# The last 256 gate and up columns of each feed-forward layer by seven products, and the decay columns in one tile

## The chip, the cores and the metric

The kernel runs on one core of a Trainium2 chip. The metric is the device time of one execution in microseconds (us): 586.07 us as the median of 3 runs (585.33 to 586.32). A profile of one execution stands beside it; its rows are those quoted below. The engines are PE (TensorE, matrix products), PEld (its weight loads), DVE (VectorE), ACT (ScalarE), POOL (GpSimd) and SP (SyncE, which here only starts transfers).

## The reference: what is computed

Two layers on 256 tokens of width 1024 in float32. Layer 0 mixes tokens by gated linear attention: one product with `w_in` gives queries, keys, values, a gate and 16 low-rank columns `gk_low`; `log_sigmoid(gk_low @ w_gk + b_gk) / 16` is the decay. Layer 1 mixes by softmax attention. Both end alike:

```python
def swiglu_ffn(x, w_gu, w_down):
    gate, up = jnp.split(x @ w_gu, 2, axis=-1)
    return (jax.nn.silu(gate) * up) @ w_down

x = layer_norm(DEEPNORM_ALPHA * x + y, ln_g[i, 0], ln_b[i, 0])
x = layer_norm(DEEPNORM_ALPHA * x + swiglu_ffn(x, ffn_w_gu[i], ffn_w_down[i]), ln_g[i, 1], ln_b[i, 1])
```

The hidden width is 2816, so `w_gu` has 2816 gate and 2816 up columns and `w_down` has 2816 rows (22 blocks of 128, called d0 to d21).

## The kernel before

**Split numbers.** A float32 matrix is held as a rounded high part (name ending in `h`, a CAST of ACT) and a low part (ending in `l`, a TENSOR_TENSOR subtraction of DVE). A product takes three matmuls: high by high, low by high, high by low (`mm3`, L301 to L303). So each 512 KB weight tile costs one pass of ACT and one of DVE over 128x1024 beside its matmuls.

**Who sets the order.** Every operation is handed to a small planner (`Plan`, L64). It has a cost for each operation, gives each weight tile one of 41 slots and each product one of 8 PSUM banks, plays the engines forward, and writes the program in the order that comes out. On the chip each engine then follows its own list in that order and waits on semaphores. A load on SP's queue waits until the last reader of its slot is done.

**A feed-forward layer** (`ffn`, L468) goes through the hidden columns in six blocks, `"PSSSSH"`. `P` (`plain`) and `S` (`seven`) take 512 gate and 512 up columns. `seven` sees the 256 tokens and the 1024 inputs as 2x2 halves and forms the products in Strassen's manner: seven half products instead of eight, named A to G after their weight tiles, 12 matmuls of 512 columns for each of a tile's two units. Its price is on DVE: three sums of weights (`add_to`, L571), and one sum that a transfer from POOL's queue makes while it lands (`add_dma`, L577). The tokens come out as rows, so a result is transposed on PE (L316) before the down product. `H` (`half`, L620) takes the last 256 gate and up columns: four weight tiles g50, g51, u50, u51, 96 matmuls of 256 columns that give the result already transposed, no sums.

**The down product** adds each of d0 to d21 onto four banks: `fy00`, `fy01` (tokens 0 to 127, the two halves of the output) and `fy10`, `fy11` (tokens 128 to 255). Rows of a block are added while the next block runs (`down_now`). Those of the last `S` block (d16 to d19) wait with those of `H` (d20, d21) for the end: all six for the first tokens, the layer norm of these on DVE, all six for the others, the second layer norm.

**The decay columns** (L728 to L740): the 16 columns of `gk_low` lie in two tiles, high and low, padded with zeros to 128 columns per input block, and take 24 matmuls of 256 columns. The sum is copied to `gkT`, to which row 16 (ones, for the bias) belongs.

**The start of layer 0**, after the decay: keys and queries (`gk0`, `gk1`, `gq`), then `qd` = queries times decay (L793, DVE), scores `sc` (L832, PE), a POOL copy of `qd` into `kx` (L815), and the cross scores `scx` (L842, PE), which wait for that copy.

Of the kernel before, what the change touches and what calls it, by code (L numbers as in the profile page):

```python
# [16 lines left out]
P = 128  # L17
# [174 lines left out]
def kernel(ctx, tc, x, positions, gla_w_in, gla_w_gk, gla_b_gk, gla_norm_g, gla_w_out,  # L192
# [31 lines left out]
    wgk = fixed("wgk", (GLA_RANK + 1, 512))  # L224
    gkT = fixed("gkT", (GLA_RANK + 1, S))
# [84 lines left out]
    def transpose_split(src, dst, t, half, skey=None, dstf=None, dkey=None, n=4, keep=None):  # L310
# [13 lines left out]
        def hi():  # L324
            nc.scalar.copy(view(0), ps.f.rearrange("p (k c) -> p k c", k=4))  # L325

        def lo():
            h, l = view(0), view(1)
            nc.vector.tensor_tensor(out=l, in0=ps.f.rearrange("p (k c) -> p k c", k=4), in1=h.bitcast(F32),  # L329
                                    op=ALU.subtract)  # L330
        kh = dkey if dkey is not None else (t, half)
        if dstf is None:
            act(512, hi, [ps], [(dst, ("h",) + kh)], urgent=True)
            dve(512, lo, [ps, (dst, ("h",) + kh)], [(dst, ("l",) + kh)], urgent=True)
# [133 lines left out]
    def ffn(i, xs, T, gb, dstT, last, x32):  # L468
# [6 lines left out]
        def down(k, t, bufs, f, ws, hfs=(0, 1)):  # L475
# [6 lines left out]
            pe(3 * 512 * len(hfs), g, list(bufs) + list(ws), [y[t][hf] for hf in hfs])  # L482
# [30 lines left out]
        def down_now(items):  # L513
            for k, bufs, f in items:
                ws = w_row(f"d{k}", wd, k)
                for t in range(2):
                    down(k, t, bufs, f, ws)

        def plain(b, c0, pend):
# [16 lines left out]
            return [(c0 // P + k, (h, l), lambda j=k: (hv(h)[:, j, :], hv(l)[:, j, :])) for k in range(4)]  # L536

        def seven(b, c0, pend):
# [3 lines left out]
            e1, e2 = S_("e1"), S_("e2")  # L542

            def product(ps, left, ws, first, last_):
                st, rd = lhs(left)
                for q, (wh, wl) in enumerate(ws):
                    def f(q=q, wh=wh, wl=wl):
                        for j in range(2):
                            sh, sl_ = st(2 * q + j)
                            cs = slice(512 * j, 512 * j + 512)  # L550
                            nc.tensor.matmul(ps.f, sh, wh.r[:, cs], start=first and q == 0 and j == 0, stop=False,  # L551
# [569 lines left out]
```

## Time and profile before

| | |
|---|---|
| median of 3 runs | 586.07 us |
| the profiled execution | 585.35 us, span 583.6 us |
| PE busy | 572.5 us (98% of the span), 3004 matmuls |
| DVE busy | 504.6 us (86%) |
| ACT busy | 345.7 us (59%) |
| POOL busy | 42.7 us |
| granted TensorE clock | 0.997 |

The span runs from the first to the last instruction; the time of the execution has 1.75 us more around it. Busy time of PE is modelled with overlap of neighbouring matmuls, so a gap between two starts shows a wait better than the busy share does. An engine works its list in order, so an instruction that waits holds all that stand behind it.

### The profile page before, as it was taken

How to read it: one execution, taken by the hardware profiler on the slowest of the kernel's cores; microseconds unless marked ns; L12 is line 12 of the kernel's file. 1: busy time of each engine (PE TensorE's matmuls, PEld its weight loads, DVE VectorE, ACT ScalarE, POOL GpSimd, SP SyncE). 2: the span in 40 equal slices, each digit the busy share in tenths (PEclk: the TensorE clock that was granted, in tenths of full speed). 3: DMA queues.
4: the chain of work that ended last, by engine and by line, in shares of the span. 5: the costliest groups of instructions: out<-in, count | busy, mean ns of one | idle time of the engine just before them, and what ended most of it. 6: DMA issues, size and time to landing. Idle time of an engine off the chain costs nothing.

```text
span 583.6 us, 8048 instructions
## 1 busy us (share of the span) xinstructions
PE 572.5 (98%) x3004; PEld 488.4 (84%) x3004; DVE 504.6 (86%) x626; ACT 345.7 (59%) x457; POOL 42.7 (7%) x39
## 2 busy tenths in 40 slices
PE   9999999999999999999999999999999999999994
PEld 8898888888878888889889999788888788888983
DVE  5899467698999999999894789888989999999926
ACT  5886465345858586876353365634595767586410
POOL 1015000010010101000000000000101000010001
PEclk9999999999999999999999999999999999999998
DMA  9984286348797877887376545626867787978201
GB/s 291 344 301 168 74 263 242 109 126 239 247 222 219 259 240 240 219 301 249 103 245 199 153 149 166 216 73 216 212 202 223 206 285 177 316 177 291 78 0 72
DMA packets 56377, 118.30 MB, mean 203 GB/s; under 512 B 5217, under 2 KB 9729, under 8 KB 56338
## 3 DMA queue, kind: packets, MB, share of 16 engines
q1 hardware_dynamic: 51554, 108.81, 55.9%
q0 software_dynamic: 4352, 8.39, 8.8%
q10 hardware_dynamic: 432, 0.59, 0.3%
q8 instruction: 23, 0.38, 0.3%
q14 instruction: 16, 0.13, 0.1%
HBM read 116.72 MB, written 1.05 MB: 202 GB/s over the span
## 4 chain that ended last, share of the span: by engine, by line
PE 75%; DVE 12%; DMA 6%; issue 3%; ACT 2%; DVEq 0%; SPq 0%; ACTq 0%
PE fy L303 6%; PE fy L301 6%; PE fy L302 6%; PE pa L554 3%; PE pa L553 3%; PE pa L551 3%; DMA d0r<-in_ffn_w_down 2%; PE y L303 2%; PE y L301 2%; PE y L302 2%; PE tr L316 2%; DVE A L571 2%; PE pc L554 2%; PE pc L551 2%; PE pc L553 2%
## 5 line engine op out<-in xcount | busy, mean ns | idle before, releaser
L571 DVE TENSOR_TENSOR A<-A,X 128x1024 f32<-128x1024 f32 x48 | 57.2, 1219 | 0.0
L577 POOL DMA_DIRECT2D X<-in_ffn_w_gu x16 | 19.6, 1263 | 206.4 <-DVE e L609 63.7
L325 ACT CAST xT<-tr 128x512 fp32r<-128x512 f32 x16 | 9.2, 590 | 32.2 <-PE tr L316 32.1
L372 POOL TENSOR_TENSOR st<-st,mhalf 128x1 f32<-128x1 f32 x8 | 7.6, 956 | 260.3 <-DVE st L370 260.3
L509 ACT CAST B0h<-A 128x1024 fp32r<-128x1024 f32 x8 | 8.4, 1053 | 9.3 <-DVE A L571 9.2
L360 DVE SCALAR_TENSOR_TENSOR r<-xn,fy 128x512 f32<-128x512 f32 x8 | 5.5, 686 | 9.7 <-PE fy L303 9.7
L509 ACT CAST C0h<-X 128x1024 fp32r<-128x1024 f32 x8 | 8.4, 1052 | 8.8 <-DMA X<-in_ffn_w_gu 8.8
L329 DVE TENSOR_TENSOR xT<-tr,xT 128x512 fp32r<-128x512 f32 x16 | 10.8, 685 | 1.3 <-ACT xT L325 0.7
L614 ACT ACTIVATE e<-pa 128x512 f32<-128x512 f32 x8 | 4.8, 599 | 11.8 <-PE pa L554 11.7
L509 ACT CAST A0h<-A 128x1024 fp32r<-128x1024 f32 x8 | 8.4, 1051 | 5.5 <-DMA A<-in_ffn_w_gu 5.4
L364 DVE BATCH_NORM_STATS2 st<-r 128x6 f32<-128x512 f32 x16 | 11.1, 693 | 0.5
L316 PEld LDWEIGHTS tr<-ident,e 128*128 128x128 f32 x64 | 7.6, 140 | 4.7 <-DVE e L615 1.9
L316 PE MATMUL tr<-ident,e 128*128 128x128 f32 x64 | 9.8, 275 | 1.7 <-DVE e L615 1.0
L382 DVE SCALAR_TENSOR_TENSOR xn<-r,st,lnb 128x512 f32<-128x512 f32 x16 | 11.3, 746 | 0.0
L509 ACT CAST C1h<-X 128x1024 fp32r<-128x1024 f32 x8 | 8.4, 1051 | 4.8 <-DMA X<-in_ffn_w_gu 4.4
L378 DVE SCALAR_TENSOR_TENSOR r<-r,st,lng 128x512 f32<-128x512 f32 x16 | 11.2, 744 | 0.0
L509 ACT CAST G0h<-A 128x1024 fp32r<-128x1024 f32 x8 | 8.4, 1050 | 4.5 <-DVE A L571 4.5
L934 DVE SCALAR_TENSOR_TENSOR og<-o,ss,sg 128x256 f32<-128x256 f32 x8 | 3.6, 478 | 8.5 <-ACT sg L896 8.5
L509 ACT CAST D0h<-A 128x1024 fp32r<-128x1024 f32 x8 | 8.4, 1053 | 3.1 <-DVE A L571 3.1
L560 ACT COPY e<-pa 128x512 f32<-128x512 f32 x16 | 9.3, 580 | 1.0 <-PE pa L554 0.9
L510 DVE TENSOR_TENSOR G1l<-A,G1h 128x1024 fp32r<-128x1024 f32 x8 | 9.8, 1222 | 0.1
L509 ACT CAST A1h<-A 128x1024 fp32r<-128x1024 f32 x8 | 8.4, 1052 | 2.4 <-DMA A<-in_ffn_w_gu 2.4
(1050 smaller groups left out, 2283.2 us busy)
## 6 DMA issues: line engine op xcount, KB each, us to landing
X<-in_ffn_w_gu SPq DMA_DIRECT2D x48, 512.0 KB, 5.0
A<-in_ffn_w_gu SPq DMA_DIRECT2D x16, 512.0 KB, 4.4
X<-in_ffn_w_gu POOLq DMA_DIRECT2D x16, 512.0 KB, 7.5
lng<-in_ln_g SPq DMA_DIRECT2D x4, 512.0 KB, 3.8
lnb<-in_ln_b SPq DMA_DIRECT2D x4, 512.0 KB, 6.1
x<-in_x SPq DMA_DIRECT2D x4, 256.0 KB, 4.6
fg00r<-in_ffn_w_gu SPq DMA_DIRECT2D x2, 512.0 KB, 7.0
fg01r<-in_ffn_w_gu SPq DMA_DIRECT2D x2, 512.0 KB, 8.3
```

The source lines that it names most:

```text
L301: nc.tensor.matmul(ps, lh, rh, start=start, stop=False)
L302: nc.tensor.matmul(ps, ll, rh, start=False, stop=False)
L303: nc.tensor.matmul(ps, lh, rl, start=False, stop=stop)
L316: nc.tensor.transpose(ps.f[:, j * P:(j + 1) * P], src.f[:, k * P:(k + 1) * P], ident.f)
L378: nc.vector.scalar_tensor_tensor(out=r.f[:, sl], in0=r.f[:, sl], scalar=st.f[:, 12:13], in1=g.f[:, sl], op0=ALU.subtract, op1=ALU.mult)
L382: nc.vector.scalar_tensor_tensor(out=xn.f[:, sl], in0=r.f[:, sl], scalar=st.f[:, 15:16], in1=b.f[:, sl], op0=ALU.mult, op1=ALU.add)
L509: act(1024, lambda: nc.scalar.copy(hi.r, raw.f), [raw], [hi])
L551: nc.tensor.matmul(ps.f, sh, wh.r[:, cs], start=first and q == 0 and j == 0, stop=False, skip_group_check=True)
L553: nc.tensor.matmul(ps.f, sl_, wh.r[:, cs], start=False, stop=False, skip_group_check=True)
L554: nc.tensor.matmul(ps.f, sh, wl.r[:, cs], start=False, stop=last_ and q == 1 and j == 1, skip_group_check=True)
L571: dve(1024, lambda q=q, other=other: nc.vector.tensor_tensor(out=raws[q].f, in0=raws[q].f, in1=other.f, op=ALU.add), [raws[q], other], [ra ...
L577: nc.gpsimd.dma_start(uv(raws[q]), unit(kh, gu, q, c0), accum_op=ALU.add)
```

## The change

- `half` is gone; the sixth block is a `seven` with `n = 256`: one unit per product, four input blocks of 256 columns in a tile. That makes 7 products of 12 matmuls of 256 columns, seven splits of weight tiles and three sums instead of four splits, and one more accumulating transfer per layer.
- With `final`, the down rows d16 to d19 are added for the first tokens between the products, and for the other tokens at the end (`later`).
- The decay columns have their high part in columns 0 to 15 and their low part in columns 16 to 31 of one tile; 16 matmuls; `wgk` and `gkT` have 33 rows, with `gla_w_gk` twice. One more small load.

```diff
@@ def seven(b, c0, pend, n=512, final=False)
+            units, nk = n // 256, 1024 // n
+            lo_, hi_ = slice(0, n), slice(512, 512 + n)
...
                 for q, (wh, wl) in enumerate(ws):
                     def f(q=q, wh=wh, wl=wl):
-                        for j in range(2):
+                        for j in range(nk):
...
-                            cs = slice(512 * j, 512 * j + 512)
+                            cs = slice(n * j, n * j + n)
-                    pe(6 * 512, f, rd + [wh, wl], [ps])
+                    pe(3 * nk * (n + 14 * (n < 512)), f, rd + [wh, wl], [ps])
...
-            down_now(pend[:2])
+            down_now(pend[:2], final)
...
+        later = []
+
+        def down_now(items, final=False):
             for k, bufs, f in items:
                 ws = w_row(f"d{k}", wd, k)
-                for t in range(2):
+                for t in range(1 if final else 2):
                     down(k, t, bufs, f, ws)
+                if final:
+                    later.append((k, bufs, f, ws))
...
-        for b, kind in enumerate("PSSSSH"):
+        for b, (kind, n) in enumerate((("P", 512), ("S", 512), ("S", 512), ("S", 512), ("S", 512), ("S", 256))):
...
         for t in range(2):
             for hf in range(2):
-                for k, bufs, f in pend:
-                    down(k, t, bufs, f, ws[k], (hf,))
+                for k, bufs, f, ws in (later + new if t else new):
+                    down(k, t, bufs, f, ws, (hf,))
...
     def loads0():
-        nc.sync.dma_start(wgk.f[0:GLA_RANK, :], gla_w_gk[0])
+        for i in range(2):
+            nc.sync.dma_start(wgk.f[i * GLA_RANK:(i + 1) * GLA_RANK, :], gla_w_gk[0])
...
+    act(1024, lambda: nc.scalar.copy(wg_hl.r, wg_r.f), [wg_r], [wg_hl])
+    dve(P, lambda: nc.vector.tensor_tensor(out=wgv(wg_hl.r, GLA_RANK), in0=wgv(wg_r.f, 0), in1=wgv(wg_hl.f, 0),
+                                           op=ALU.subtract), [wg_r], [wg_hl])
...
         for k in range(KT):
-            mm3(ps, wv[0][:, k, :], wv[1][:, k, :], T0.ap[0][:, :, k, :], T0.ap[1][:, :, k, :], k == 0, k == KT - 1)
-    pe(24 * 256, fgk, [T0, wg_h, wg_l], [gkps])
+            for i in range(2):
+                nc.tensor.matmul(ps, wv[:, k, :], T0.ap[i][:, :, k, :], start=k == 0 and i == 0,
+                                 stop=k == KT - 1 and i == 1)
+    pe(16 * 270, fgk, [T0, wg_hl], [gkps])
```

Outside three places the planner's order on PE, DVE and SP stays as it was: the start of layer 0, the sixth block with the entry to what follows it, once in each layer. In those places it moves as follows (names are the program's, with buffer numbers).

DVE at the start of layer 0, before: `wv1*l` and `wg0*l` are low parts of weight tiles that PE needs later, `qd` feeds the scores.

```order
L266 TENSOR_TENSOR wv13l_571<-wv13r_409,wv13h_550 128x1024
L266 TENSOR_TENSOR wg00l_589<-wg00r_413,wg00h_569 128x1024
L793 SCALAR_TENSOR_TENSOR qd_607<-gq_0_451,ep_483 128x512
L266 TENSOR_TENSOR wg01l_609<-wg01r_449,wg01h_573 128x1024
L793 SCALAR_TENSOR_TENSOR qd_607<-gq_0_468,ep_483 128x512
L266 TENSOR_TENSOR wg02l_629<-wg02r_481,wg02h_587 128x1024
L813 TENSOR_TENSOR kx_513<-qd_607,ep_483 128x4x64
L266 TENSOR_TENSOR wg03l_644<-wg03r_508,wg03h_605 128x1024
L835 TENSOR_TENSOR sc_0_657<-sc_0_635,imask 128x512
```

The same place after:

```order
L266 TENSOR_TENSOR wv13l_575<-wv13r_399,wv13h_554 128x1024
L775 SCALAR_TENSOR_TENSOR qd_595<-gq_0_437,ep_487 128x512
L775 SCALAR_TENSOR_TENSOR qd_595<-gq_0_456,ep_487 128x512
L266 TENSOR_TENSOR wg00l_607<-wg00r_417,wg00h_573 128x1024
L795 TENSOR_TENSOR kx_517<-qd_595,ep_487 128x4x64
L266 TENSOR_TENSOR wg01l_619<-wg01r_454,wg01h_577 128x1024
L266 TENSOR_TENSOR wg02l_632<-wg02r_473,wg02h_593 128x1024
L817 TENSOR_TENSOR sc_0_652<-sc_0_623,imask 128x512
L817 TENSOR_TENSOR sc_0_652<-sc_0_636,imask 128x512
```

Both `qd` instructions now stand ahead of `wg00l` and `wg01l`, and the first mask of the scores (`sc`) stands behind `wg02l`.

DVE in the sixth block of layer 1, before: `g50l`, `g51l`, `u50l`, `u51l` are the four low parts of `H`; `e` and `G0l`, `G1l` belong to the fifth block.

```order
L266 TENSOR_TENSOR g50l_4970<-g50r_4903,g50h_4914 128x1024
L603 TENSOR_TENSOR e_0_4829<-pc_4831,e_0_4829 128x512
L605 TENSOR_TENSOR e_0_4829<-e_0_4829 128x512
L510 TENSOR_TENSOR G0l_4996<-A_0_4647,G0h_4960 128x1024
L609 TENSOR_TENSOR e_0_4863<-e_0_4863,pa_4801 128x512
L510 TENSOR_TENSOR G1l_5007<-A_0_4655,G1h_4983 128x1024
L266 TENSOR_TENSOR g51l_5024<-g51r_4922,g51h_4926 128x1024
L329 TENSOR_TENSOR hT4l_5036<-tr_5009,hT4h_5022 128x4x128
L266 TENSOR_TENSOR u50l_5038<-u50r_4942,u50h_4944 128x1024
L266 TENSOR_TENSOR u51l_5052<-u51r_4949,u51h_4957 128x1024
L266 TENSOR_TENSOR d16l_5060<-d16r_4968,d16h_4972 128x1024
```

The same place after: `A0l`, `C0l`, `B0l` are low parts of the sixth block, L577 its sums of weights.

```order
L510 TENSOR_TENSOR A0l_4974<-A_0_4928,A0h_4930 128x1024
L609 TENSOR_TENSOR e_0_4839<-pc_4841,e_0_4839 128x512
L611 TENSOR_TENSOR e_0_4839<-e_0_4839 128x512
L510 TENSOR_TENSOR G0l_4996<-A_0_4657,G0h_4964 128x1024
L615 TENSOR_TENSOR e_0_4871<-e_0_4871,pa_4811 128x512
L510 TENSOR_TENSOR G1l_5007<-A_0_4665,G1h_4976 128x1024
L577 TENSOR_TENSOR A_0_4928<-A_0_4928,X_0_4948 128x1024
L329 TENSOR_TENSOR hT4l_5033<-tr_5011,hT4h_5024 128x4x128
L510 TENSOR_TENSOR C0l_5038<-X_0_4959,C0h_4961 128x1024
L510 TENSOR_TENSOR B0l_5046<-A_0_4928,B0h_5035 128x1024
L266 TENSOR_TENSOR d16l_5058<-d16r_4984,d16h_4993 128x1024
L577 TENSOR_TENSOR A_0_4928<-A_0_4928,X_0_4972 128x1024
```

Ten passes of 128x1024 for the products of the sixth block (seven low parts, three sums) now stand where four stood, with the low parts of d16 to d21 between them.

PE in the sixth block of layer 1, before, where the last matmuls of `H` (`gu`) end and the down rows begin:

```order
L302 MATMUL gu_5108<-xT_0_3741,u51l_5052 128x256
L303 MATMUL gu_5108<-xT_1_3742,u51h_4957 128x256
L301 MATMUL fy_0_4108<-d16h_4972,hT4h_5022 128x512
L302 MATMUL fy_0_4108<-d16h_4972,hT4l_5036 128x512
L303 MATMUL fy_0_4108<-d16l_5060,hT4h_5022 128x512
L301 MATMUL fy_0_4108<-d17h_4994,hT4h_5022 128x512
L302 MATMUL fy_0_4108<-d17h_4994,hT4l_5036 128x512
L303 MATMUL fy_0_4108<-d17l_5068,hT4h_5022 128x512
```

After, from the end of product F to the down row d19, with `e` the fifth tile of tokens to be transposed:

```order
L560 MATMUL pa_5073<-F0l_5166,s3hl_3902 128x256
L301 MATMUL fy_0_4118<-d18h_5056,hT4h_5024 128x512
L302 MATMUL fy_0_4118<-d18h_5056,hT4l_5033 128x512
L303 MATMUL fy_0_4118<-d18l_5136,hT4h_5024 128x512
L301 MATMUL fy_0_4119<-d18h_5056,hT4h_5024 128x512
L302 MATMUL fy_0_4119<-d18h_5056,hT4l_5033 128x512
L303 MATMUL fy_0_4119<-d18l_5136,hT4h_5024 128x512
L316 MATMUL tr_5216<-ident,e_0_5109 128x128 x2
L301 MATMUL fy_0_4118<-d19h_5068,hT4h_5024 128x512
L302 MATMUL fy_0_4118<-d19h_5068,hT4l_5033 128x512
L303 MATMUL fy_0_4118<-d19l_5156,hT4h_5024 128x512
```

The down rows d16 to d19 stand two by two behind the products D and F (`fy_0_4118` and `fy_0_4119` are the two banks of the first tokens), and a transpose of two blocks of 128 is new.

## Rows read from the trace of the kernel before

**Rows 1.** The page: busy us (share of the span) and instructions.
```profile
PE 572.5 (98%) x3004; PEld 488.4 (84%) x3004; DVE 504.6 (86%) x626; ACT 345.7 (59%) x457; POOL 42.7 (7%) x39
```

**Rows 2.** The largest of PE's waits: engine, tile, line, releaser; total, times, longest.
```profile
PE junk L680 <- DVE zeros L673: 1.1, 1, 1.1
```

**Rows 3.** Stretches of `gu` matmuls, both layers: length, busy (count), clock, DMA share, GB/s.
```profile
264.06:276.00 11.94, 11.75 (x96) 11.52 (x95) 0.34 (x1) 0.37 (x1) 1.00 0.78 259
547.77:559.52 11.75, 11.56 (x96) 11.32 (x95) 0.42 (x1) 0.39 (x1) 1.00 0.01 2
```

**Rows 4.** The stretch of the decay matmuls, same columns as rows 3.
```profile
19.37:22.24 2.87, 2.87 (x25) 2.87 (x24) 0.00 (x0) 1.00 1.04 381
```

**Rows 5.** Four transposes in the chain that ended last: start us, us, count.
```profile
256.94 0.44 PE tr L316 x4
```

**Rows 6.** DVE, sixth block of layer 1: start us, us, instruction, [idle <- releaser].
```profile
541.13 1.22 DVE L266 TENSOR_TENSOR g51l<-g51r,g51h 128x1024 fp32r<-128x1024 f32 x1
542.36 0.69 DVE L329 TENSOR_TENSOR hT4l<-tr,hT4h 128x512 fp32r<-128x512 f32 x1
542.97 1.22 DVE L266 TENSOR_TENSOR u50l<-u50r,u50h 128x1024 fp32r<-128x1024 f32 x1
544.10 1.22 DVE L266 TENSOR_TENSOR u51l<-u51r,u51h 128x1024 fp32r<-128x1024 f32 x1
...
557.31 0.42 DVE L643 TENSOR_TENSOR sil<-gu,sil 128x256 f32<-128x256 f32 x1 [3.63 <-ACT sil L641]
```

**Rows 7.** DVE in layer 0: a 256-wide operation and the next start.
```profile
275.66 0.42 DVE L643 TENSOR_TENSOR sil<-gu,sil 128x256 f32<-128x256 f32 x1
275.99 1.22 DVE L266 TENSOR_TENSOR mv11l<-mv11r,mv11h 128x1024 fp32r<-128x1024 f32 x1
```

**Rows 8.** PE's first two matmuls of the down rows, layer 1.
```profile
559.52 0.39 PE L301 MATMUL fy<-d16h,hT4h 128*128 128x512 f32 x1
559.75 0.39 PE L302 MATMUL fy<-d16h,hT4l 128*128 128x512 f32 x1
```

**Rows 9.** Two loads of the next mixer in layer 0: SP's issues.
```profile
258.79 0.38 SPq L262 DMA_DIRECT2D mv00r<-in_moba_w_in  x1
264.25 0.37 SPq L262 DMA_DIRECT2D mv10r<-in_moba_w_in  x1
```

**Rows 10.** ACT's casts of these two loads.
```profile
263.19 1.05 ACT L265 CAST mv00h<-mv00r 128x1024 fp32r<-128x1024 f32 x1 [1.29 <-DMA mv00r<-in_moba_w_in]
270.56 1.05 ACT L265 CAST mv10h<-mv10r 128x1024 fp32r<-128x1024 f32 x1 [0.26 <-DMA mv10r<-in_moba_w_in]
```

**Rows 11.** PE's timeline at the scores.
```profile
50.13 0.33 PE L832 MATMUL sc<-qd,ka 128*128 128x64 f32 x2
...
51.53 0.44 PE L832 MATMUL sc<-qd,ka 128*128 128x64 f32 x2 [0.40 <-DVE qd L793]
...
54.03 0.39 PE L832 MATMUL sc<-qd,kb 128*128 128x64 f32 x2
54.40 1.16 PE L842 MATMUL scx<-kx 128*128 128x128 f32 x8
```

**Rows 12.** DVE at the scores.
```profile
47.93 1.21 DVE L266 TENSOR_TENSOR wg00l<-wg00r,wg00h 128x1024 fp32r<-128x1024 f32 x1
49.07 0.67 DVE L793 SCALAR_TENSOR_TENSOR qd<-gq,ep 128x512 f32<-128x512 f32 x1
...
54.01 0.67 DVE L835 TENSOR_TENSOR sc<-sc,imask 128x512 int32<-128x512 int32 x1
```

**Rows 13.** POOL's copies there.
```profile
41.66 1.07 POOL L808 COPY kb<-ke 128x256 f32<-128x256 f32 x2 [0.46 <-DVE ke L787]
42.68 6.72 POOL L812 COPY kx<-ke 128x256 f32<-128x256 f32 x1
51.54 2.81 POOL L815 COPY kx<-qd 128x256 f32<-128x256 f32 x1 [2.13 <-DVE qd L793]
```

**Rows 14.** The accumulating transfers (L577), all 16 of them.
```profile
DMA to landing us min/median/max: 5.7/7.5/9.7
```

More of the change, by code (lines that the diff above doesn't have):

```diff
@@ L565, in get @@
                 if (kh, gu) not in have:
-                    have[kh, gu] = [load_unit(f"X{q}", unit(kh, gu, q, c0)) for q in range(2)]
+                    have[kh, gu] = [load_unit(f"X{q}", unit(kh, gu, q, c0, n), n) for q in range(units)]
                 return have[kh, gu]
@@ L606, in seven @@
                                                      op=ALU.mult), [(e1, 0), (e1, 1)], [(e1, 0)], urgent=True)
-            transpose_split(e1, (h, l), 0, 0, skey=0, dkey=0, dstf=lambda i: dst(i, slice(0, P)))
-            product(pa, "s3", [split_unit(f"F{q}", have[0, 1][q]) for q in range(2)], False, False)
-            dve(512, lambda: nc.vector.tensor_tensor(out=e2.f[:, 0:512], in0=e2.f[:, 0:512], in1=pa.f,
+            transpose_split(e1, (h, l), 0, 0, skey=0, dkey=0, n=n // P, dstf=lambda i: dst(i, slice(0, P)))
@@ L610, in seven @@
+            product(pa, "s3", [split_unit(f"F{q}", have[0, 1][q]) for q in range(units)], False, False)
+            dve(n, lambda: nc.vector.tensor_tensor(out=e2.f[:, lo_], in0=e2.f[:, lo_], in1=pa.f[:, lo_],
                                                      op=ALU.subtract), [pa, (e2, 0)], [(e2, 0)], urgent=True)
-            down_now(pend[2:])
+            down_now(pend[2:], final)
             add_to(ch, 1, 0)
-            product(pa, "a11", [split_unit(f"G{q}", ch[q]) for q in range(2)], False, True)
@@ L653, in ffn @@
+            transpose_split(e2, (h, l), 1, 1, skey=1, dkey=1, n=n // P, dstf=lambda i: dst(i, slice(P, 2 * P)))
+            return [(c0 // P + j, lambda t: [(h, t), (l, t)], lambda j=j: (hv(h)[:, j, :], hv(l)[:, j, :])) for j in range(n // P)]
         c0, pend = 0, []
-        for b, kind in enumerate("PSSSSH"):
+        for b, (kind, n) in enumerate((("P", 512), ("S", 512), ("S", 512), ("S", 512), ("S", 512), ("S", 256))):
             if kind == "S" and not sums:
                 sums.update(x_sums(x32))
-            final = kind == "H" and c0 + 256 == HID
-            new = {"P": plain, "S": seven, "H": half}[kind](b, c0, [] if final else pend)
-            pend = pend + new if final else new
-            c0 += 256 if kind == "H" else 512
+            pend = plain(b, c0, pend) if kind == "P" else seven(b, c0, pend, n, c0 + n == HID)
+            c0 += n
@@ L661, in ffn @@
         assert c0 == HID
[L662 removed]
+        new = [(k, bufs, f, w_row(f"d{k}", wd, k)) for k, bufs, f in pend]
         xn = []
```

131 lines of the change are left out of this document (50 added, 81 removed).

## The prediction, made before the changed kernel ran

> **What bounds the kernel now.** I read the page's busy line first, then the waits of PE, then the stretches that the change touches, on PE's timeline and on DVE's beside it. PE is busy for 98% of the span, DVE for 86% [rows 1]. The largest wait of PE is 1.1 us at the very start [rows 2]; the sixth blocks have none, and the start of layer 0 has one of 0.4 us for `qd`, shown below. So almost everywhere the end moves with the number and size of matmuls, and the question for each edit is whether DVE, ACT and the loads keep ahead of a PE that has less to do. The granted clock is 1.00, the 2.4 GHz level, in all three stretches [rows 3, 4]; nothing here empties PE for long, so I leave it there.
>
> **The sixth block on PE.** The 96 `gu` matmuls and four transposes fill 11.94 us in layer 0 and 11.75 us in layer 1 [rows 3]. Four transposes take 0.44 us [rows 5], so a matmul of 256 columns costs (11.94 - 0.44) / 96 = 0.120 us in layer 0 and 0.118 us in layer 1. The trace has no matmul with tokens as weights and 256 columns of `w_gu` moving, but `gu` has the same two shapes with the operands exchanged, so I take its price. Seven products need 84: twelve fewer, -1.44 and -1.41 us. The two results must be transposed, two blocks each: four transposes, +0.44 us per layer. The down rows only change place. That leaves -1.00 us in layer 0 and -0.97 us in layer 1 while nothing waits.
>
> **The same block on DVE.** Ten passes of 128x1024 instead of four, at 1.13 us from start to start [rows 6], are +6.8 us; seven operations of 256 elements (five sums and products, two low parts) instead of four, at 0.33 us from start to start [rows 7], are +1.0 us. PE must not feel these 7.8 us, so I walk the two lists of layer 1 side by side in the times of before, with 0.6 us for an operation of 512 elements (`hT4l` to `u50l`) [rows 6]. The order is the same up to G1l, which still ends at 541.13, where g51l starts now [rows 6]. Then: sum for B 542.3, hT4l 542.9, C0l 544.0, B0l 545.2, d16l 546.3, sum for D 547.4, d17l 548.6, the fifth block's last `e` 549.2, E0l 550.4, D0l 551.5, d18l 552.6, hT4l 553.2, `e` 553.6, d19l 554.7, F0l 555.8, sum for G 557.0, d20l 558.1, two `e` 558.8, G0l 559.9. PE begins at 547.77 [rows 3] and takes 1.41 us for each product: A and B to 550.6, four transposes, C to 552.45, D to 553.9, two down rows to 556.7 (12 matmuls of 512 columns at 0.23 from start to start [rows 8]), E to 558.1, F to 559.5, two more rows with two transposes to 562.5, G. So D0l is 0.9 us early, F0l 2.3, G0l 2.6. After G the rows d20 and d21 of the first tokens cover the result's way through ACT, DVE and PE, and 36 matmuls for the other tokens cover the first layer norm, as now. DVE's extra work fits, because DVE stood idle 3.63 us and more behind d21l [rows 6]. I take no wait in layer 1: -0.97. If DVE comes 1 us later than that, the gain is gone; below -1.0 nothing more is to be had, since no matmul beyond the twelve goes.
>
> **The entry to the attention of layer 1.** In layer 0 DVE and ACT are also splitting the next weights. The same walk gives the same leads there. By it DVE's low parts for the first value products come just in time: mv10l ends 0.3 us before its first matmul, and PE's list has one more ready product (mv00 of the second tokens) ahead of mv12. The first layer norm ends 1 us earlier, like PE. What is tight is ACT's list: the cast `hT5h`, which releases d20, stands behind `mv10h`, and the last silu behind `mv11h`. Their loads now wait for slots that F0l and d20l give back, near 272.1 and 274.4. A load of this kind took 4.4 us from issue to cast (mv00) and 6.3 us (mv10) [rows 9, 10]. With 4.4 nothing waits; with 6.3 PE stands about 0.5 us before d20 or the last transposes. I take +0.2: -0.8 for layer 0, from -1.0 to, with a load of 8 us, +1.2.
>
> **The decay.** 24 matmuls filled 2.87 us [rows 4]; 16 take 1.91: -0.96. DVE's split of 128x1024 becomes one of 128 columns, -0.9 us on an engine that PE does not wait for here; the extra small load delays SP by about half a microsecond, and the weight tiles behind it are used several microseconds after they are split. `pre` moves behind 12 more matmuls, and ACT reaches its result no earlier than now. Both cost nothing.
>
> The 0.96 us arrive at the scores, where something else ends last. PE starts `sc` at 50.13, waits 0.40 us for the second `qd`, goes on in steps of 0.227 us (eleven from 51.53 to 54.03), ends near 54.26 and starts `scx` at 54.40 [rows 11]. With the decay shorter it reaches `sc` at 49.17. DVE is through with wv13l at 47.93, where wg00l starts [rows 12], and both `qd` stand there now, to 49.1 (0.6 each). So `sc` runs through without a wait, and PE would be at `scx` by 49.17 + 16 x 0.227 = 52.8, 1.6 us earlier. But `scx` needs POOL's copy. That copy (L815) ran 2.81 us and the one before it (L812) 6.72 us, where two copies of that size took 1.07 us together [rows 13]. Both long ones came to their end inside an operation of DVE that reads PSUM: L812 at 49.40 within `qd` (49.07 to 49.74), L815 at 54.35 within the mask of `sc` (54.01 to 54.68) [rows 12, 13]; through the low parts of weights before them they made no end. After the change L815 can start at 49.1, and DVE's list then holds wg00l, `kx`, wg01l, wg02l (three at 1.14, one at 0.33: to 52.9) before the next operation on PSUM. If it again ends 0.34 us into the mask, that is 53.2, and `scx` starts at 53.25: -1.15 instead of -1.6. I take -1.1; if the copy is as quick as the short ones, -1.6; if it is kept for one more low part (1.14), 0.
>
> The Trainium skill, "SBUF — State Buffer", section "Who interferes with whom", says that a DVE instruction with two SBUF inputs contends with a GpSimd instruction that reads SBUF, and that the one issued first blocks the other for its whole length. By that rule the copy is shut out through wg02l, as above, and the start gives -1.1; without it -1.6. The trace agrees with the rule, 6.72 against 0.54 us for one copy of the same size, all beside two-input subtractions of DVE.
>
> **The sum.** -1.1 - 0.8 - 0.97 = -2.9 us. The profiled execution, 585.35 us (span 583.6 and 1.75 around it), would become 582.5. It is 0.7 us below the median of the runs, 586.07, and the change takes the same from both: 583.2 us.
>
> **Rivals.**
> 1. *DVE or ACT become the bound in the sixth block.* Leads of 0.3 to 2.4 us come from a walk with constant steps. For it: DVE has no free time from the fifth block's start to d21l, and each hand-over of a sum through ACT to a low part can add tenths. Against it: its steps are regular to 0.01 us [rows 6]. Price: 0.5 to 1 us in each layer; with 0.9 the sum is -2.9 + 1.8 = -1.1: 585.0 us.
> 2. *The start gives nothing*, because POOL's copy is kept longer: the sum is -1.8, 584.3 us.
> 3. *Slower: ACT's list behind the accumulating transfer.* F0h waits for the new transfer on POOL's queue, and behind it stand the first silu, the copy of D's result and G0h. Issued at 542.3, it may land 14.0 us later before G0l (F0h 1.05, then F0l, the sum for G, d20l, two `e` and G0l, 5.2 us) is late for PE at 562.5. The sixteen of now land after 5.7 to 9.7 us [rows 14], and the new one has pieces half as long, which the trace does not show for this queue. From 16.1 us on it costs 2.1 us in each layer, and the kernel is slower by over 0.2%: 583.2 + 4.2 = 587.4 us.
> 4. *More than I count*: the copy is quick and no wait comes in, -1.6 - 1.0 - 0.97 = -3.6: 582.5 us.
>
> **Chances.** The forecast 0.54, rival 1 0.18, rival 2 0.08, rival 3 0.10, rival 4 0.10. About 0.2%, 1.2 us, is what a measurement of this kernel can tell from no change (584.9 and 587.2). Faster: the forecast, rivals 2 and 4, and under half of rival 1, less a little for runs that differ by 1 us: 0.76. Same: the rest of rival 1 and of these: 0.15. Slower: rival 3 past its point: 0.09. The range leaves out rival 3 and the worst of rival 1, and below it takes in rival 4 with half a microsecond for runs that differ: 582.0 to 585.9 us.
>
> **What would show it.** 16 decay matmuls in 1.9 us; `sc` without a gap; POOL's L815 copy ending within the first mask (L817) and `scx` 1.1 us earlier. Then 84 matmuls of 256 columns at 0.118 to 0.120 us per layer, no wait of PE before D, F or G, DVE without its 3.6 us of idle time behind d21l. I am wrong if these matmuls are dearer than `gu`, if PE waits for a low part or a transpose in the sixth block, or if F0h waits for its transfer.

## The result, and the profile after

The changed kernel took 581.51 us (median of 6 runs, 580.57 to 582.81), the kernel before 585.36 us beside it (6 runs, 584.31 to 586.32): 3.85 us less, ratio 0.994 with a 95% interval of 0.9923 to 0.9957. Forecast were 2.9 us less and 583.2 us, with a range from 582.0 to 585.9. So the direction was right, the gain larger than forecast, and the time 0.5 us below the range. The profiled execution took 580.57 us, the shortest of the six; its span is 578.8 us.

The busy line of the page and the waits of PE (in total, times, longest), which answer to [rows 1, 2]:

```profile
PE 568.6 (98%) x2980; PEld 485.6 (84%) x2980; DVE 518.8 (90%) x644; ACT 352.5 (61%) x469; POOL 45.3 (8%) x41
```

```profile
PE junk L651 <- DVE zeros L644: 1.1, 1, 1.1
PE tr L316 <- DVE e L621: 1.0, 2, 0.6
PE scx L824 <- POOL kx L797: 0.4, 1, 0.4
```

DVE has 14 us more to do, and PE waits less than before. The wait for `qd` is gone, and the one for POOL's copy has come in its place.

**Where the time went.** The same instruction is found on PE's timeline in both kernels, and the difference of its two starts says how much has been gained up to there. The second pair of columns is a second profile of each kernel, unaltered (runs e3_after2 and e4_before2 below).

| stretch on PE | forecast | first pair | second pair |
|---|---|---|---|
| start to `scx` | -1.1 | -1.26 | -1.29 |
| `scx` to the sixth block of layer 0 | 0 | -0.60 | +0.10 |
| sixth block of layer 0, to the first `mv00` product | -0.8 | -0.90 | -0.40 |
| first `mv00` product to the last `po` | 0 | -0.94 | -1.04 |
| last `po` to the sixth block of layer 1 | 0 | -0.24 | +0.11 |
| sixth block of layer 1 to the end of PE | -0.97 | -0.79 | -0.82 |
| sum | -2.87 | -4.73 | -3.34 |

The three places of the change give 2.95 and 2.51 us. What is left over has two parts: one stretch in the attention of layer 1, about 1 us in both pairs, and stretches that go either way.

**The start.** PE's decay matmuls and `scx`, POOL's copy, and DVE beside it (start us, us, instruction), which answer to [rows 4, 11 to 13]:

```profile
19.23 2.08 PE L718 MATMUL gk<-xT,wgkhl 128*128 128x256 f32 x16
...
53.14 1.16 PE L824 MATMUL scx<-kx 128*128 128x128 f32 x8 [0.44 <-POOL kx L797]
```

```profile
49.15 3.94 POOL L797 COPY kx<-qd 128x256 f32<-128x256 f32 x1 [0.99 <-DVE qd L775]
```

```profile
49.02 1.20 DVE L266 TENSOR_TENSOR wg00l<-wg00r,wg00h 128x1024 fp32r<-128x1024 f32 x1
50.15 0.41 DVE L795 TENSOR_TENSOR kx<-qd,ep 128x256 f32<-128x256 f32 x1
50.48 1.21 DVE L266 TENSOR_TENSOR wg01l<-wg01r,wg01h 128x1024 fp32r<-128x1024 f32 x1
51.62 1.20 DVE L266 TENSOR_TENSOR wg02l<-wg02r,wg02h 128x1024 fp32r<-128x1024 f32 x1
52.75 0.67 DVE L817 TENSOR_TENSOR sc<-sc,imask 128x512 int32<-128x512 int32 x1
```

The next matmuls start at 21.14, 1.91 us behind the first of the decay. The copy runs through three low parts and a product (`kx`) and ends at 49.15 + 3.94 = 53.09, which is 0.34 us into the mask, as in the kernel before. `scx` starts 0.05 us later.

**The sixth block.** Stretches from its first matmul, in layer 0 to the first `mv00` product and in layer 1 to the end of PE's work, of before and of after (length, busy and count by engine, clock, DMA share, GB/s):

```profile
264.06:293.28 29.22, 29.22 (x182) 26.24 (x180) 26.36 (x34) 13.38 (x19) 0.99 (x1) 1.00 0.57 186
547.77:575.64 27.87, 27.87 (x173) 25.08 (x171) 14.42 (x22) 2.77 (x6) 0.93 (x1) 1.00 0.05 20
```

```profile
262.20:290.52 28.32, 28.32 (x173) 25.17 (x172) 27.18 (x37) 18.84 (x27) 1.00 (x1) 1.00 0.78 260
543.83:570.91 27.08, 27.08 (x164) 24.10 (x163) 22.33 (x32) 8.26 (x14) 0.93 (x1) 1.00 0.17 61
```

PE is busy through all of both. Two matmuls of product B (seven steps apart) and a new pair of transposes among the down rows of d19, then the first matmul of D, F and G beside DVE's low parts for them, in layer 1:

```profile
545.72 0.28 PE L559 MATMUL pc<-B0h,s1hl 128*128 128x256 f32 x1
...
546.56 0.28 PE L560 MATMUL pc<-B0l,s1hl 128*128 128x256 f32 x1
...
548.54 0.28 PE L557 MATMUL pa<-D0h,s2hl 128*128 128x256 f32 x1
...
554.16 0.28 PE L557 MATMUL pa<-F0h,s3hl 128*128 128x256 f32 x1
...
556.99 0.38 PE L316 MATMUL tr<-ident,e 128*128 128x128 f32 x2
557.13 0.48 PE L301 MATMUL fy<-d19h,hT4h 128*128 128x512 f32 x1
557.44 0.39 PE L302 MATMUL fy<-d19h,hT4l 128*128 128x512 f32 x1
...
558.60 0.28 PE L557 MATMUL pa<-G0h,xT 128*128 128x256 f32 x1
```

```profile
546.84 1.22 DVE L510 TENSOR_TENSOR D0l<-A,D0h 128x1024 fp32r<-128x1024 f32 x1
...
551.17 1.22 DVE L510 TENSOR_TENSOR F0l<-X,F0h 128x1024 fp32r<-128x1024 f32 x1
...
555.60 1.22 DVE L510 TENSOR_TENSOR G0l<-A,G0h 128x1024 fp32r<-128x1024 f32 x1
```

In product B a matmul of 256 columns takes 0.84 / 7 = 0.120 us. The pair of transposes costs 0.14 us, and 0.08 more at the matmul behind it (0.31 us to the next start instead of 0.23). If each matmul is charged from its start to the next one's, the 84 of the products took 10.04 us where the 96 `gu` took 11.39, the transposes 0.62 instead of 0.35, and the down rows 16.41 instead of 16.12: -1.35 + 0.27 + 0.29 = -0.79. (A full block of seven has six matmuls of 512 columns for each unit, twelve for a product, not twelve for each unit as the description of the kernel before has it.) The low parts end 0.5 us (D), 1.8 (F) and 1.8 (G) before the first matmul of their product.

**The attention of layer 1.** The stretch from the first `mv00` product to the last `po`, before and after:

```profile
293.28:380.99 87.71, 87.30 (x599) 80.11 (x598) 71.35 (x132) 47.83 (x90) 0.99 (x1) 1.00 0.57 181
```

```profile
290.52:377.29 86.77, 86.77 (x599) 80.27 (x598) 78.29 (x138) 48.19 (x90) 0.99 (x1) 1.00 0.56 184
```

In it, the load `fg00r` (the first gate weights of the feed-forward layer behind it; the last figure is the us from issue to landing), its cast on ACT, and PE's wait, in the kernel before:

```profile
fg00r<-in_ffn_w_gu SPq DMA_DIRECT2D x1, 512.0 KB, 7.8
```

```profile
368.12 1.05 ACT L265 CAST fg00h<-fg00r 128x1024 fp32r<-128x1024 f32 x1 [4.78 <-DVE ms L1016]
```

```profile
PE pt L1044 <- DVE pr L1035: 0.3, 1, 0.3
```

The load and its cast after (the wait is gone):

```profile
fg00r<-in_ffn_w_gu SPq DMA_DIRECT2D x1, 512.0 KB, 6.5
```

```profile
364.04 1.05 ACT L265 CAST fg00h<-fg00r 128x1024 fp32r<-128x1024 f32 x1 [3.44 <-DMA fg00r<-in_ffn_w_gu]
```

On ACT the casts `fg00h` and `fg01h` stand ahead of the exponentials of the softmax (`pr`). `fg00r` is issued on SP's queue 1.4 us after `lng` and 0.4 us after `lnb`, 512 KB each, which are not needed until the last norm, 200 us later. The cast comes 4.08 us earlier on the clock, 1.3 us earlier against PE. The releaser named for the first cast, `ms`, had long been done; it is the load.

**Layer 0, second block** (the expectations below call it the third). The transposes between the two halves of the down row d2, before and after:

```profile
163.25 0.63 PE L316 MATMUL tr<-ident,e 128*128 128x128 f32 x4 [0.60 <-DVE e L605]
```

```profile
161.41 0.63 PE L316 MATMUL tr<-ident,e 128*128 128x128 f32 x4
```

In both profiles the chain that ended last runs from the landing of `d0r` through ACT and DVE to this `e`. `d0r` landed 7.34 us after its issue before, 6.77 after, and the 0.6 us are that. The fourteen profiles in which this load has its old place bear it out: the wait is what the landing takes beyond 6.75 us (up to 6.77 us: none; 7.00: 0.25; 7.67: 0.92).

### The profile page after: what moved, and what is told of

The parts are those of the page before. It is cut to its first block, busy times and chain, and to the rows that moved or that the text cites. A ratio compares the mean times of both kernels' runs of the same rounds, so it can differ in the third digit from the quotient of the medians.

```text
span 578.8 us, 8048 instructions
## 1 busy us (share of the span) xinstructions
PE 568.6 (98%) x2980; PEld 485.6 (84%) x2980; DVE 518.8 (90%) x644; ACT 352.5 (61%) x469; POOL 45.3 (8%) x41
## 3 DMA queue, kind: packets, MB, share of 16 engines
HBM read 117.81 MB, written 1.05 MB: 205 GB/s over the span
## 4 chain that ended last, share of the span: by engine, by line
PE 76%; DVE 9%; DMA 7%; ACT 3%; issue 3%; POOL 1%; DVEq 0%; ACTq 0%; SPq 0%
PE fy L303 6%; PE fy L301 6%; PE fy L302 6%; PE pa L560 4%; PE pa L559 4%; PE pa L557 4%; PE y L303 3%; PE y L302 3%; PE y L301 3%; DMA d0r<-in_ffn_w_down 2%; PE tr L316 2%; PE pc L557 2%; PE pc L560 2%; PE pc L559 2%; DVE A L577 2%
## 5 line engine op out<-in xcount | busy, mean ns | idle before, releaser
L577 DVE TENSOR_TENSOR A<-A,X 128x1024 f32<-128x1024 f32 x54 | 64.4, 1217 | 0.0
L583 POOL DMA_DIRECT2D X<-in_ffn_w_gu x18 | 22.2, 1261 | 261.2 <-PE fy L302 90.5
L620 ACT ACTIVATE e<-pa 128x512 f32<-128x512 f32 (+1 forms) x10 | 5.5, 555 | 11.5 <-PE pa L560 11.5
L510 DVE TENSOR_TENSOR D0l<-A,D0h 128x1024 fp32r<-128x1024 f32 x10 | 12.2, 1219 | 0.0
L510 DVE TENSOR_TENSOR G0l<-A,G0h 128x1024 fp32r<-128x1024 f32 x10 | 12.2, 1218 | 0.0
L510 DVE TENSOR_TENSOR A0l<-A,A0h 128x1024 fp32r<-128x1024 f32 x10 | 12.2, 1218 | 0.0
L510 DVE TENSOR_TENSOR E0l<-X,E0h 128x1024 fp32r<-128x1024 f32 x10 | 12.2, 1218 | 0.0
L510 DVE TENSOR_TENSOR F0l<-X,F0h 128x1024 fp32r<-128x1024 f32 x10 | 12.2, 1218 | 0.0
L510 DVE TENSOR_TENSOR C0l<-X,C0h 128x1024 fp32r<-128x1024 f32 x10 | 12.2, 1217 | 0.0
L510 DVE TENSOR_TENSOR B0l<-A,B0h 128x1024 fp32r<-128x1024 f32 x10 | 12.2, 1216 | 0.0
```

What stands on the lines that cost most here:

```text
L510: dve(1024, lambda: nc.vector.tensor_tensor(out=lo.r, in0=raw.f, in1=hi.f, op=ALU.subtract), [raw, hi], [lo])
L577: dve(1024, lambda q=q, other=other: nc.vector.tensor_tensor(out=raws[q].f, in0=raws[q].f, in1=other.f, op=ALU.add), [raws[q], other], [ra ...
L583: nc.gpsimd.dma_start(uv(raws[q], n), unit(kh, gu, q, c0, n), accum_op=ALU.add)
```

## Experiments

Each kernel was timed on one chip in turn with the kernel before; ratios are to that. The runs `e`, `f`, `g` and `h` had a chip each, on which the kernel before took 585.18, 585.34, 585.89 and 584.95 us.

**The two parts alone.** `e1_decay` has the decay of the changed kernel and the sixth block of before, `e2_seven` the reverse.

```diff
# e1_decay: before, with
+    wg_r, wg_hl = S_("wgkr"), S_("wgkhl", True)
...
+    pe(16 * 270, fgk, [T0, wg_hl], [gkps])
# e2_seven: the changed kernel, with
+    pe(24 * 256, fgk, [T0, wg_h, wg_l], [gkps])
```

> Only the decay columns in one tile; the sixth block stays as it was. Theory A (the parts are worth what PE's rows say, and the rest of the 4.8 us between the two profiles is the landing time of two loads, d0r in layer 0 and fg00r in layer 1, which varies from run to run in either kernel): scx starts 1.1 to 1.3 us earlier than in before (54.40), and the median is 1.1 to 1.3 us below that of before, up to 0.6 more or less as d0r lands. Theory B (the change itself takes those waits away, by the phase in which the loads meet other work): the wait of the transposes for e in the third block of layer 0 (0.6 us) is gone here too, whenever it is profiled, and the median is 1.7 to 1.9 us below.

> Only the sixth block by seven products with the down rows between them, in both layers; the decay as before. Theory A: 84 matmuls and eight transposes instead of 96 and four, 0.9 us less in each layer on PE, no new wait there; the median 1.8 us below before, and the profile has the old waits or not by the landing of d0r and fg00r. Theory B: the start is that of before, so the 0.6 us wait in the third block of layer 0 is there, but the wait for the softmax rows (0.34 us, and 0.9 us in all in that stretch) is gone: 2.4 to 2.7 us below before.

With the decay alone: 583.81 us against 585.18, ratio 0.9966 (0.995 to 0.9983), -1.4 us, which lies between the two theories. From the first decay matmul to `scx` 33.84 us instead of 35.03. With seven products alone: 584.13, ratio 0.998 (0.9961 to 0.9999), -1.05; the sixth blocks were 0.91 and 0.79 us shorter, but `d0r` landed after 7.67 us and PE waited 0.92 us for it in that profile. Both theories missed the seven products: A said 1.8, B 2.4 to 2.7. The two parts add up to 2.4, the whole change gives about 4. In the profile with the decay alone `fg00r` landed after 9.2 us, and PE paid for it:

```profile
PE pt L1055 <- DVE pr L1046: 1.8, 1, 1.8
```

**Both kernels again, unaltered.**

> The changed kernel once more, unaltered, for a second profile. Theory A: d0r's way from issue to cast differs from the 6.8 us of the first profile by some tenths, and with it the wait of the transposes for e; the same for fg00r (6.6 us) and the softmax; the span is 579 to 581 us. Theory B: both stretches look as in the first profile, no wait for e in the third block of layer 0, span 578.8 within 0.3 us. Median 2.9 to 3.9 us below before by either.

> The kernel before once more, unaltered, for a second profile. Theory A: d0r's 7.3 us from issue to cast and fg00r's 7.9 us are one draw of many; here they differ by some tenths, and the waits of 0.6 us (e, layer 0) and 0.34 us (softmax) shrink or grow with them; span 582.5 to 584. Theory B: the two waits are there again, with the same sizes within 0.1 us. Median within 0.5 us of before by either.

581.06 us for the changed kernel, ratio 0.9915 (0.989 to 0.994); 585.11 for the kernel before, ratio 0.9997. Neither theory holds for all. `d0r` behaves as A says: the wait in the second block was 0.60 and 0.25 us in the kernel before, none and 0.37 after. `fg00r` does not: 7.8 and 7.9 us in the kernel before, 6.5 and 6.5 in the changed one. The -0.40 us of layer 0 in the second pair is ACT's list, as the prediction feared, though behind another load than it named (ACT, DVE, PE):

```profile
273.53 1.05 ACT L265 CAST mv02h<-mv02r 128x1024 fp32r<-128x1024 f32 x1 [1.70 <-DMA mv02r<-in_moba_w_in]
...
275.56 1.23 DVE L510 TENSOR_TENSOR G0l<-A,G0h 128x1024 fp32r<-128x1024 f32 x1 [1.56 <-ACT G0h L509]
...
281.24 0.44 PE L316 MATMUL tr<-ident,e 128*128 128x128 f32 x2 [0.25 <-DVE e L621]
```

The cast `G0h` stands behind `mv02h`, which waits for its load; G0l, d21l and the last `e` come later, and PE waits. Of the eight profiles with seven products and the rows between them, `f1` and `h1` lost as much (28.73 and 28.81 us), in `f1` with ACT waiting 1.42 us for `mv11r`, a load that the prediction named; the five others took 28.3 us.

**The loads of layer 1 exchanged** on SP's queue, all else as it was, in the changed kernel (`f1`), in the kernel before (`f2`), and with the decay alone (`g4`).

```diff
+        for nm in ("lnb11", "lng11"):
+            o = next(x for x in order if x.eng == "SP" and x.bufs and x.bufs[0].name == nm)
+            order.remove(o)
...
+            order.insert(i + 1, o)      # i: the load fg01r
```

> The changed kernel, in which SP issues the loads fg00r and fg01r of layer 1 ahead of lng and lnb (the scale and shift of the last layer norm, used 200 us later) instead of behind them; all engines keep their order. Theory A (the attention stretch is longer in the kernels with the old sixth block only because fg00r, behind two other loads, lands late by draw, and its cast stands ahead of the softmax on ACT): fg00h starts 3.5 to 5.5 us after its issue instead of 6.6, the stretch from the first mv00 product to the last po stays at 86.8 us as in both profiles of the changed kernel (which had no wait there), and the median is that of the changed kernel within 0.3 us. Theory B (it is the order of PE in that stretch that differs): the same here, no change; the two part at the next kernel.

> The kernel before with the same exchange of loads. Theory A: fg00h starts 3.5 to 5.5 us after its issue instead of 7.9, the wait for the softmax rows is gone, the stretch from mv00 to the last po falls from 87.7 to about 86.8 us, and the median is 0.8 to 1.0 us below that of before. Then the kernel with seven products, with the same exchange, is 2.9 us faster than this one, which is the sum that was predicted. Theory B: the stretch stays at 87.7 and the median within 0.3 us of before.

> Only the decay columns in one tile (the sixth block as before), with the loads fg00r and fg01r of layer 1 ahead of lng and lnb. Theory A (the two parts of the change did not add up because with the decay alone fg00r landed 9.2 us after its issue and PE waited 1.8 us for the softmax): the stretch from mv00 to the last po is 86.8 us instead of 89.1, and the median is 1.3 to 2.2 us below the kernel with the decay alone: 581.8 to 582.5. Rival (the loss is elsewhere): 583.5 to 584.

In all three `fg00r` landed after 3.5 or 3.6 us, and the stretch from `mv00` to the last `po` was 86.77 us, to the hundredth that of the changed kernel. The kernel before goes to 584.6 (ratio 0.9985, 0.9966 to 1.0004, -0.7 us), the changed one stays at 581.19 (ratio 0.9914, 0.9888 to 0.9939), the decay alone goes to 583.0 (ratio 0.9952, 0.9933 to 0.997; it was 583.81 on another chip, and 1.3 us less were expected at least). `f1` and `f2` ran side by side: with this load out of the way the whole change gives 3.4 us there, where 2.9 were expected. How they divide between the decay and the seven products (1.6 and 1.8 by the plain medians, against 1.1 and 1.77 forecast) is known to about half a microsecond only, because `g4` ran on another chip.

**The down rows behind product G**, so that they cover nothing.

```diff
-            down_now(pend[:2], final)
...
+            if final:
+                down_now([(k, lambda t, bufs=bufs: bufs(t) + [pa], f) for k, bufs, f in pend], True)
```

> The changed kernel with the down rows d16 to d19 of the first tokens held until product G is done, in both layers; the planner orders the rest around that. Same matmuls, same splits. Theory A (DVE's ten passes need the rows as cover, but only just): PE waits for F0l and G0l, 0.5 to 1 us in each layer, 1 to 2 us in all, and the median is 1 to 2 us above the changed kernel, still below before. Theory C (the rows cover nearly all of DVE's extra 7.8 us): 2.5 us and more in each layer, slower than before. Theory D (DVE is ahead anyway): within 0.3 us of the changed kernel.

586.77 us, ratio 1.0013 (0.9993 to 1.0034): the sixth blocks take 30.97 and 29.10 us instead of 28.32 and 27.08. That is 2.65 and 2.02 us, between A and C, and the change is lost. Not all of it is DVE's ten passes: in each layer 0.68 us are a wait of product G for `e`, DVE's operation on the result of F, which has to leave the bank `pa` first. PE in layer 0:

```profile
271.98 0.39 PE L560 MATMUL pa<-F0l,s3hl 128*128 128x256 f32 x1 [0.35 <-DVE F0l L510]
...
274.33 0.36 PE L557 MATMUL pa<-G0h,xT 128*128 128x256 f32 x1 [0.68 <-DVE e L616]
...
275.37 0.38 PE L560 MATMUL pa<-G0l,xT 128*128 128x256 f32 x1 [0.57 <-DVE G0l L510]
```

**The order on DVE at the start.** `f6`: the changed kernel, the first mask ahead of `wg01l`. `g3`: the kernel before, both `qd` ahead of `wg00l`.

```diff
+        for nm in ("wg02l", "wg01l"):          # f6; g3: ("wg01l", "wg00l") behind the second qd
+            o = find("DVE", nm)
+            order.remove(o)
+            order.insert(order.index(mask) + 1, o)
```

> The changed kernel with one DVE instruction moved at the start of layer 0: the first mask of the scores, which reads PSUM, now stands ahead of the low parts wg01l and wg02l instead of behind them. Theory A (POOL's copy into kx comes to its end only inside a DVE instruction that reads PSUM): the copy, which ran 3.94 us, ends at about 51.2 instead of 53.09, scx follows the scores at 52.7 without a wait, and the kernel is 0.4 us faster. Theory E (the copy needs that long beside any DVE work): it ends at 53.1 as now, no gain.

> The kernel before (24 decay matmuls) with one exchange on DVE: both qd ahead of wg00l and wg01l, as in the changed kernel. Theory A (the end of the start is set by POOL's copy, which DVE's order moves): the scores run without a wait, scx starts 0.6 us earlier against the decay's first matmul (34.4 us behind it instead of 35.0 to 35.3), half of what the decay change gave there; the median 0.5 us below before. Theory F (the start of the kernel before loses clock in some executions because PE waits between the two halves of the scores): with that wait gone none of the executions has a granted clock below 0.995, where about a third of before have. If the lower clock comes from something else in the start, a quarter to a third of the executions have it here too.

`f6` (POOL, DVE, PE):

```profile
48.72 1.67 POOL L804 COPY kx<-qd 128x256 f32<-128x256 f32 x1 [0.99 <-DVE qd L782]
...
49.72 0.41 DVE L802 TENSOR_TENSOR kx<-qd,ep 128x256 f32<-128x256 f32 x1
50.80 0.69 DVE L824 TENSOR_TENSOR sc<-sc,imask 128x512 int32<-128x512 int32 x1 [0.67 <-PE sc L821]
...
52.39 0.89 PE L831 MATMUL scx<-kx 128*128 128x128 f32 x6
```

The copy ends at 50.39, in the 0.67 us in which DVE is idle before the mask. So it takes no operation on PSUM to let it through: a pause of DVE does it too. The Trainium skill, "SBUF — State Buffer", section "Who interferes with whom", says that a DVE instruction with at most one SBUF input, outside some of its modes, does not contend with GpSimd; the copies that end within `qd` and the mask, each with one input in PSUM, agree. Not every break is enough: in the kernel before a TENSOR_SCALAR on one SBUF tile (`rope`, 45.40, 0.33 us) stands between two of the subtractions beside L812, and that copy did not end there. `scx` follows the scores without a wait. The time did not move (581.65, ratio 0.9921, 0.9892 to 0.995): in its profile `d0r` was late, and PE waited 0.8 us for `e` in the second block.

`g3` (POOL, PE):

```profile
49.44 5.08 POOL L822 COPY kx<-qd 128x256 f32<-128x256 f32 x1 [0.99 <-DVE qd L800]
...
54.57 0.60 PE L849 MATMUL scx<-kx 128*128 128x128 f32 x3 [0.92 <-POOL kx L822]
```

The copy starts 2.1 us earlier than before and ends no earlier, because DVE now has four low parts and a product ahead of its first mask. 585.47 us, ratio 0.9989 (0.9974 to 1.0005); half a microsecond had been expected. So the order of `qd` alone gives nothing at `scx`; in the changed kernel the copy has three low parts to outlast instead of four, and by `f6`, too, it is the place of the mask that counts.

**Scale and shift of the second norm late.** `g1`: in the changed kernel they are loaded ahead of the fifth block. `g2`: the same with the mask of `f6`. `h3`: the kernel before with this edit.

```diff
-    gb = load_ln(1, 1)
...
+            if b == 4:
+                gb = load_ln(i, 1)
```

> The changed kernel, but the scale and shift of each layer's second norm are loaded ahead of the fifth block instead of before the feed-forward layer: two of the 41 slots are free for weights through most of it, and the planner loads them earlier. Theory A (in layer 0 the fourth down row waits for DVE's chain behind the landing of d0r, 0 to 0.9 us by draw, and the softmax of layer 1 for fg00r): both waits are gone, and the kernel is 0.5 to 1 us faster than the changed one: 580.5. Rival: the slots are not what holds the loads, no gain within 0.3 us.

> The same with the first mask of the scores ahead of wg01l and wg02l. Alone the mask took the wait of scx away (0.44 us), but its profile lost that again to the wait behind d0r. Theory A: with d0r early the 0.4 to 0.6 us of the start arrive at the end: 580.0, 0.4 us below the kernel without it. Rival: something else ends last before the first block of seven, no difference.

> The kernel before, with scale and shift of each layer's second norm loaded ahead of the fifth block, as in the fastest kernel so far (which has the change too, 579.0). Theory A (beside the three places of the change, the gain is what late loads cost the kernel before): with the loads out of the way in both, the two differ by the places alone, 2.9 to 3.2 us: 581.9 to 582.2. Rival (the change gives more by itself): 583 and above.

`g1` took 578.99 us, ratio 0.9883 (0.986 to 0.9905), and `g2` 578.7, ratio 0.9879 (0.9856 to 0.9903): both faster than either kernel, and more than expected of them (4 runs each); the 0.3 us between the two are less than their intervals. `fg00r` lands after 3.7 or 3.8 us, and no wait for it is left. That alone is not the gain, since `f1` had none; what the free slots and what the earlier loads give, no run separates. `h3` took 583.82, ratio 0.9979 (0.9961 to 0.9997), 1.6 to 1.9 us over what theory A said. Its three places differ from `g1` by 1.00, 0.94 and 0.80 us, as before. Most of the rest is in the fourth block of seven in layer 1, where PE waited once:

```profile
518.05 0.66 PE L316 MATMUL tr<-ident,e 128*128 128x128 f32 x4 [1.75 <-DVE e L615]
```

This is `fg00r`'s story again: the silu behind that `e` stands on ACT behind the cast of `d13r`, for which ACT waited 5.14 us. The load landed 7.9 us after its issue, in the sixteen other profiles after 3.2 to 4.9. Whether the late landing belongs to the kernel or to that execution, one profile does not say.

**Another place in SBUF.** Four pairs of slots exchanged, so that the four loads lie where they lie in the other kernel: in the changed kernel (`h1`) and in the kernel before (`h2`).

```diff
+SWAP = {3: 8, 8: 3, 15: 20, 20: 15, 29: 34, 34: 29, 14: 37, 37: 14}
```

> The changed kernel with four pairs of SBUF slots exchanged throughout, so that lng, lnb, fg00r and fg01r of layer 1 lie where they lie in the kernel before; every engine keeps its order. Theory S (the place of these tiles in SBUF decides how fast the four loads run): lnb lands after 6.6 to 7.1 us and fg00r after 7.7 to 7.9 us, as in the kernel before, instead of 5.5 and 6.5. Theory P (not the place): lnb after 5.5 to 6.4, fg00r after 6.5 to 7.4, as in the kernels with seven products so far. The time within 0.7 us of the changed kernel by either.

> The kernel before with the same exchange, so that these four tiles lie where they lie in the changed kernel. Theory S: lnb after 5.5 to 6.4 us, fg00r after 6.5 to 7.1, the wait for the softmax rows gone or under 0.2 us. Theory P: lnb after 6.6 to 7.1, fg00r after 7.7 to 9.2, a wait of 0.3 us and more.

`h1`, then `h2`, the landing of `fg00r`:

```profile
fg00r<-in_ffn_w_gu SPq DMA_DIRECT2D x1, 512.0 KB, 6.4
```

```profile
fg00r<-in_ffn_w_gu SPq DMA_DIRECT2D x1, 512.0 KB, 8.3
```

The place does not decide it (581.9 and 584.89 us). With `fg00r` in its old order, the five profiles with the old sixth block now have 7.7, 7.8, 7.9, 8.3 and 9.2 us, the six with seven products 6.4, 6.5, 6.5, 6.7, 7.1 and 7.4. What does decide it stays open: SP's issues stand at the same distances, and PE's work around them is the same. One thing differs that no experiment moved. In the kernel before, between the issue of `lng` and the landing of `fg00r`, there is one packet of a queue whose kind the profile gives as instruction (queue, packets, MB, share of 16 engines):

```profile
q8 instruction: 1, 0.02, 0.7%
```

It has 16 KB and takes 0.97 us, where the packets of the loads take 0.13 on average. In all five profiles with the old sixth block one starts while `fg00r` is under way; of the six with seven products only `e2` has it there, and in the others it comes after the landing. With it `fg00r` took 7.1 to 9.2 us, without it 6.4 to 7.4. With the loads exchanged, `lnb` landed after 8.3 and 8.4 us with such a packet (`f2`, `g4`) and after 7.1 without (`f1`). So the packet is a candidate for the difference; that it is the cause is not shown, and `f6` has 7.4 us without it.

## Why the prediction fell short

**The start: right.** -1.1 forecast, -1.26 and -1.29 measured, -1.11 and -1.25 from the first decay matmul on. The mechanism held in each kernel: the copy ends when DVE comes to an operation with an input in PSUM or pauses, and where `scx` waits for the copy it follows within 0.06 us. One reading was too simple: the long copy L812 did not run beside subtractions of two tiles alone (`rope` stood among them), and the two short ones ran beside two-input operations as well, of 32 partitions and 0.4 to 0.5 us (`rr`); the quickest copies of this size took 0.39 us.

**The sixth block: right, with two sizes off.** Layer 1: -0.79 and -0.82 for -0.97. The products gave 1.35 us instead of 1.41, and the four new transposes took 0.44 with the delay behind them, as forecast. The rest, 0.12 us, is in the sentence that the down rows only change place: they now begin behind products and transposes, where the first steps take 0.23 to 0.24 us instead of 0.227. Layer 0: -0.90 or -0.40 for -0.8, by whether a load of the next mixer holds ACT. The walk along DVE's list gave leads of 0.9, 2.3 and 2.6 us for D, F and G (the first rival says 2.4 for the largest); they were 0.5, 1.8 and 1.8, and no wait came. That the pending rows are what keeps PE from waiting, as the walk had it, is shown by taking them away: 2.65 and 2.02 us.

**The rivals.** DVE or ACT as the bound: not in layer 1, by 0.4 us in layer 0 at times. The start giving nothing: no. The accumulating transfer: issued at 538.89 in layer 1, it landed 6.1 us later and was there when ACT came to F0h, which started at 549.85 without a wait. More than I count: that the time came out near and below its 582.5 us is luck, since its mechanism was not there; the copy was no quicker than forecast.

**The step that failed** is the sentence that almost everywhere the end moves with the number and size of matmuls, by which nothing outside the three places was counted. The wait of `pt`, 0.3 us, is the last of five in the list of PE's waits, and the prediction does not mention it. The stretch from `mv00` to the last `po` takes 86.77 us in this order where nothing waits, and the kernel before lay 0.94 us above that, behind a load that a transfer not needed for 200 us holds up. With that load in its old place it came 0.3 to 2.8 us sooner in every profile with seven products than in any without. Of the wait nothing was left in four of these six; `e2` kept 0.2 us and `f6` 0.5. That it is this load is shown by the exchange on SP's queue, which takes 0.94 us from that stretch in the kernel before and nothing from the changed one; why it lands sooner with seven products is not shown.

**The level.** I added 0.7 us, because the profiled execution (585.35) lay below the median of three runs (586.07). Over 6, 29, 23, 17 and 25 runs the median was 585.36, 585.18, 585.34, 585.89 and 584.95: the profile had been typical, and the three runs lay high. Without that step the forecast would have been 582.5, and the same range 0.7 us lower would have taken in 581.51. So of the 1.7 us that it missed by, 0.7 is the level. The other 1.0 is gain that was not counted. By the profiles the stretch with the load is as large, 0.94 and 1.04 us; by the medians taking the load away gave 0.7 us, with an interval that includes nothing, so this share is less sure than the place of the wait.

## What to carry to other kernels

A wait of 0.3 us on the bottleneck is worth following to the load behind it: the landing of a load that stands behind others varies by microseconds, and a cast that waits for it holds all that stands behind it on its engine. A product with fewer matmuls pays only if other ready work for PE stands between its parts while the other engines prepare them; here that cover was worth more than the saving itself. And load last what is needed last: two tiles brought in 200 us early held up others and took two slots, and moving them gave some 2 us more (581.06 and 581.51 to 578.99, on different chips), half of what the whole change gave.

## What the runs showed of the hardware that was not expected

A POOL copy of 128x256 took 0.39 to 6.7 us by what DVE did beside it: the long ones ended 0.26 to 0.34 us after DVE's chain of operations between tiles in SBUF broke, be it by an operation on PSUM or by idle time.

In 26 of the 94 executions of the kernel before that were timed beside the experiments the mean granted clock was under 0.995, and these were some 1 to 4 us longer; of the kernels with the new decay 1 execution of 66 was so. `g3`, which has the old decay but no wait of PE between the two halves of the scores, had none in 12; beside it the kernel before had 3 in 17, so that is no proof. No trace of such an execution was taken, so where the clock fell is not known; the medians of the kernel before move by 0.1 to 0.4 us with it, that of `f2` by 0.3.
